# Low parts and taps taken off GpSimd in the recurrence stage, and modulation tasks moved from block 1 to block 1b

## The chip, the core and the metric

The kernel runs on one core of a Trainium2 chip. The metric is the device time of one execution in microseconds. A core has TensorE (PE: matmuls; PEld: its weight loads), VectorE (DVE), ScalarE (ACT), GpSimd (POOL) and SyncE (SP), which issues the DMAs here. Each engine runs its own queue in order, and semaphores join the queues.

## The reference, cut to what matters

Three blocks on a sequence of 512 tokens of 1024 channels, all in float32. The first has a pooling mixer (layer 0) and a dilated attention (layer 1), the second three mixers side by side, the third a bidirectional gated recurrence beside a 31-tap depthwise convolution, and then a convolutional FFN. The parts that the change touches:

```python
# block 1, layer 0: four groups of 512 channels, windows 2, 4, 8, 16
proj = h @ w_in;  u, gate = proj[..., :2048], proj[..., 2048:]
pooled_g = trailing_mean(u_g, w_g) - u_g
mixed_g = pooled_g @ w_grp[g]
y = (mixed * scale * silu(gate)) @ w_out

# modulation vectors: silu(c) @ w + b, for c_ctx_3, c_2 and c_3, eleven vectors of 1024 used in blocks 2 and 3

# block 3: eight heads of 128, in both directions
S_t = diag(f_t) S_{t-1} + k_t v_t^T;  o_t = S_t^T q_t        # in chunks
o = rmsnorm(o) * silu(g);  y_hg = o @ w_hg_out
u = silu(layernorm(dwconv1d(cv_a * sigmoid(cv_b), 31 taps)));  y_cv = u @ w_cv_out
```

## The kernel before, in words

Activations lie transposed: 128 channels on the partitions, 512 tokens along the row. Every product with a weight goes through `form_a` or `form_b`. Each splits weights and activations in a high part (rounded by ScalarE, L129 and L134) and a low part (the rest, a subtraction), and sums three matmuls for each pair of 128-channel tiles, so a `form_a` over 1024 channels is 24 matmuls of 128x512. The subtraction for the weights is L130, on the engine that `k.wlo` names when the weight is asked for: VectorE, or GpSimd in some stretches. Weights come by DMA from SP's queue in three buffers (`wr`), and their parts `wh` and `wl` have three buffers each, so a weight's parts can be made when the product three before has let go of its buffers.

The program is laid out by a scheduler which goes by the order of the code, with the weights' steps ahead by priority, and which may place an instruction of later code earlier where its engine would stand.

**Block 1** runs two halves of two groups each. In a group there are four input products with the trailing means on VectorE (L432 to L438), split into `pg`, then, four times, a gate product (Silu on ScalarE to `sg`) and a group product over `pg`, scaled and gated to `zt` and split into `zh` and `zl`. At the end of each half eight output products run over `z`.

**Modulation tasks** (`vec_input`, `add_vec`) are a list of 102 small jobs: 3 loads of a row vector with its Silu, and 11 vectors of 8 pieces and one finish each. A piece loads 512 KB (`gr`) and multiplies it by the row vector in four quarters on VectorE (L366). `k.bg(n)` takes the next n jobs. Block 1 calls `k.bg(1)` 24 times in each half (4 + 4 in each group, 8 in the output products), and block 1b calls `k.bg(2)` after each head of each attention pass, 32 times, which empties the list in its 27th call. The context steps (`ctx_steps`), which need the first two vectors (the first 19 jobs), begin at the sixth output product of the second half.

**Block 3's recurrence stage.** Ahead of it convolutions c0 to c3 and some products run (`BEFORE`). Then `gla_gates`, `gla_front` and `gla_back` run for heads 0 to 7, with the rest beside them (`BESIDE`: convolutions c4 to c7, gates h0 to h7 and g4 to g7). A head makes exponents of cumulated gates on VectorE and ScalarE, products of 32 to 128 columns on TensorE into `psA` and `psD`, then merges the masked diagonal parts D into A (L1165 to L1171), forms the states SS, the output O, its inverse square root (`rsqrt`, L1212) and the gated result `y`. From L1293 on `k.wlo` is GpSimd, until the last head is done. In c4 to c7 five of the 31 taps run on GpSimd (L1257, L1259), and VectorE adds their sum at the end (L1263).

Of the kernel before, what the change touches and what calls it, by code (L numbers as in the profile page):

```python
# [12 lines left out]
U8 = mybir.dt.uint8  # L13
# [396 lines left out]
def block1(k, ctx, w0, acc, x):  # L410
# [6 lines left out]
    for half in range(2):  # L417
        z = None
        for g in (2 * half, 2 * half + 1):
            w = POOL_W[g]  # L420
            k.wlo = nc.gpsimd if g == 1 else nc.vector
            pg = k.b16(F32R, shape=(P, 2, 4, S), name="pg")
            for m in range(4):
                ps = k.form_a(I["w_in_a"][4 * g + m], x, w=None if g + m else w0)
                u = k.f("upad", (P, PADW + S))
                nc.gpsimd.memset(u[:, :PADW], 0.0)
                nc.scalar.activation(u[:, PADW:], ps, AF.Copy)
                s, sh, lo = u, 1, 0
                while sh < w:
                    lo = lo + sh  # L430
                    s2 = k.f("us", (P, PADW + S))
                    nc.vector.tensor_add(s2[:, lo:], s[:, lo:], s[:, lo - sh:PADW + S - sh])  # L432
                    s, sh = s2, 2 * sh
                pl = k.f("pl")
                nc.vector.scalar_tensor_tensor(pl, s[:, PADW:], 1.0 / w, u[:, PADW:], op0=ALU.mult, op1=ALU.subtract)
                e = k.small((P, 16), "edge")
                nc.vector.tensor_mul(e[:, :w - 1], s[:, PADW:PADW + w - 1], invc[:, :w - 1])
                nc.vector.tensor_sub(pl[:, :w - 1], e[:, :w - 1], u[:, PADW:PADW + w - 1])  # L438
                k.split(pg[:, 0, m], pg[:, 1, m], pl)
                k.bg(1)  # L440
            if z is None:
                z = k.b16(F32R, name="zh"), k.b16(F32R, name="zl")
            for m in range(4):
                ps = k.form_a(I["w_in_a"][16 + 4 * g + m], x)
                sg = k.f("sg")
                end = nc.scalar.activation(sg, ps, AF.Silu)
                ps = k.form_a(I["w_grp_a"][g, m], (pg[:, 0], pg[:, 1]), kt=4)
                t = k.f("zt")
                nc.vector.scalar_tensor_tensor(t, ps, scale_a[:, 4 * g + m:4 * g + m + 1], sg, op0=ALU.mult, op1=ALU.mult)
                kk = 4 * (g % 2) + m  # L450
                k.split(z[0][:, kk], z[1][:, kk], t)
                k.bg(1)
        if half:
            k.table_after(end)
        for j in range(8):
# [9 lines left out]
            k.bg(1)  # L465
# [65 lines left out]
def block1b(k, ctx, acc, h1, x2d):  # L531
# [10 lines left out]
    for j in range(8):  # L542
# [39 lines left out]
        for g in range(2):  # L582
            po = k.ps_o((P, 2, NT, 64))
            ml.append(k.small((P, NT, 4), f"ml{g}"))
            with k.tc.high_priority(offset=(ATT_AHEAD, 0)[g]):
                for hh in range(2):
# [45 lines left out]
                    k.bg(2)  # L632
# [489 lines left out]
def gla_back(k, h, hT, V, R, q, tot, masks, gnw, DB, y):  # L1122
# [40 lines left out]
    m = lambda i, r=slice(0, P): masks[r, i:i + 1, :].to_broadcast([r.stop - r.start, NT, 32])  # L1163
# [6 lines left out]
    for b in range(4):  # L1170
        cp(A[sub(b), :, sub(b)], m(4, sub(b)), D[sub(b)])  # L1171
# [40 lines left out]
    r = k.rsqrt(ss, NT, 1.0 / P, EPS)  # L1212
# [10 lines left out]
def block3(k, hT, x3d, out):  # L1223
# [4 lines left out]
    masks = k.const.tile([P, 5, 32], U8, name="masks")  # L1228
    mf = k.f("mf", (P, 5, 32))
# [13 lines left out]
    def conv(j):  # L1243
# [8 lines left out]
        npt = 5 if j >= 4 else 0  # L1252
        if npt:
            d = k.a("cd")
            for i, t in enumerate(range(31 - npt, 31)):
                e = k.f("ce") if i else d
                nc.gpsimd.tensor_scalar(e, u[:, t:t + S], dww[:, j, t:t + 1], 0.0, op0=ALU.mult, op1=ALU.add)  # L1257
                if i:
                    nc.gpsimd.tensor_add(d, d, e)  # L1259
        for t in range(1, 31 - npt):  # L1260
            nc.vector.scalar_tensor_tensor(c, u[:, t:t + S], dww[:, j, t:t + 1], c, op0=ALU.mult, op1=ALU.add)  # L1261
        if npt:
            nc.vector.tensor_add(c, c, d)  # L1263
# [29 lines left out]
    k.wlo = nc.gpsimd  # L1293
# [149 lines left out]
def constants():  # L1443
# [19 lines left out]
    out["masks"] = np.stack([same(16) & ~same(8), same(8) & ~same(4), same(4) & (si <= ti), same(4) & (si >= ti), same(16)], 1).astype(f)  # L1463
# [83 lines left out]
```

## Time and profile before

| | us |
|---|---|
| median of 3 runs | 3278.64 (3277.37 to 3281.38) |
| the profiled execution | 3281.25 |
| its span, from the first to the last instruction | 3279.2 |
| TensorE busy | 3129.3 |
| VectorE busy | 2109.7 |
| ScalarE busy | 1234.2 |
| GpSimd busy | 452.1 |

All times from the trace count from the start of the span. A busy TensorE is not one at its peak: PEclk is the clock that it was granted, as a share of the full one. A group's mean covers what an instruction took from its start to its end, so time in which it was held up after its start is in it.

### The profile page before, as it was taken

The page shows a single profiled execution, that of the slowest core. Times are in us where ns is not written, and L with a number is a line of the kernel's source. Part 1 is how long each engine was busy: PE and PEld are TensorE (multiplying, and loading weights), DVE is VectorE, ACT ScalarE, POOL GpSimd, SP SyncE. Part 2 cuts the span into 40 slices and gives each one's busy share as a digit, 9 for nine tenths or more (in the row PEclk, how much of TensorE's full clock was granted, in tenths as well). Part 3 has the DMA queues.
Part 4 walks back from the last instruction along what each step waited for, and adds up shares of the span by engine and source line. Part 5 has one row for each costly group of instructions (what it writes and reads, how often), then busy time and mean ns, then how long its engine had stood idle before and what let it go on. Part 6 is the DMA issues. An engine that isn't in the chain of part 4 may idle for free.

```text
span 3279.2 us, 44923 instructions
## 1 busy us (share of the span) xinstructions
PE 3129.3 (95%) x17460; PEld 2567.1 (78%) x17460; DVE 2109.7 (64%) x4077; ACT 1234.2 (38%) x2085; POOL 452.1 (14%) x372
## 2 busy tenths in 40 slices
PE   9799999999999899999999999989879888989998
PEld 7688878787877787777778988888666666878886
DVE  8846764646454735545443363699887788788777
ACT  4233543434343533334442233432454351433332
POOL 1300000000000301100110011221422433110000
PEclk9899999999999999999999999999899999999999
DMA  8523342333222431211122222433212213423332
GB/s 289 197 96 123 112 133 97 127 102 124 96 94 67 122 99 65 67 62 65 52 81 96 91 90 97 135 122 113 70 65 72 82 54 126 151 75 96 97 94 84
DMA packets 112772, 334.35 MB, mean 102 GB/s; under 512 B 17584, under 2 KB 22704, under 8 KB 112560
## 3 DMA queue, kind: packets, MB, share of 16 engines
q1 hardware_dynamic: 112560, 331.50, 30.6%
q8 instruction: 137, 2.24, 0.3%
q14 instruction: 75, 0.61, 0.1%
HBM read 316.77 MB, written 14.68 MB: 101 GB/s over the span
## 4 chain that ended last, share of the span: by engine, by line
PE 39%; DVE 14%; issue 2%; ACT 1%; DVEq 0%; ACTq 0%
PE mm L145 11%; PE mm L144 11%; PE mm L143 11%; DVE cy L1261 5%; PE O L883 1%; DVE wl L130 1%; PE S L867 1%; PE S L1159 1%; PE T L876 1%; PE mm L172 1%; PE mm L174 1%; PE mm L173 1%; DVE KD L1136 0%; DVE A L1171 0%; DVE R L1110 0%
## 5 line engine op out<-in xcount | busy, mean ns | idle before, releaser
L129 ACT ACTIVATE wh<-wr 128x1024 fp32r<-128x1024 f32 (+3 forms) x505 | 504.2, 1000 | 1107.5 <-PE mm L144 798.9
L130 DVE TENSOR_TENSOR wl<-wr,wh 128x1024 fp32r<-128x1024 f32 (+2 forms) x403 | 484.9, 1204 | 422.4 <-ACT wh L129 418.6
L130 POOL TENSOR_TENSOR wl<-wr,wh 128x1024 fp32r<-128x1024 f32 x102 | 257.6, 2530 | 697.5 <-ACT wh L129 652.5
L143 PE MATMUL mm<-h2h,wh 128*128 128x512 f32 (+1 forms) x776 | 310.0, 400 | 1.0 <-ACT th L675 0.9
L145 PE MATMUL mm<-h2h,wl 128*128 128x512 f32 (+1 forms) x776 | 309.8, 399 | 0.0
L144 PE MATMUL mm<-h2l,wh 128*128 128x512 f32 (+1 forms) x776 | 309.6, 399 | 0.0
L144 PE MATMUL mm<-h1l,wh 128*128 128x512 f32 x512 | 212.6, 415 | 1.7 <-DVE h1l L318 1.4
L143 PE MATMUL mm<-h1h,wh 128*128 128x512 f32 x512 | 206.8, 404 | 0.5 <-ACT h1h L317 0.5
L145 PE MATMUL mm<-h1h,wl 128*128 128x512 f32 x512 | 207.0, 404 | 0.0
L144 PE MATMUL mm<-h3l,wh 128*128 128x512 f32 x512 | 204.6, 412 | 1.5 <-DVE h3l L318 1.5
L143 PE MATMUL mm<-h3h,wh 128*128 128x512 f32 x512 | 204.6, 413 | 1.4 <-DVE kk L1001 1.4
L145 PE MATMUL mm<-h3h,wl 128*128 128x512 f32 x512 | 205.5, 414 | 0.0
L1261 DVE SCALAR_TENSOR_TENSOR cy<-uc,dww,cy 128x512 f32<-128x512 f32 x220 | 200.1, 915 | 4.5
L143 PEld LDWEIGHTS mm<-h2h,wh 128*128 128x128 f32 (+1 forms) x776 | 146.0, 188 | 27.7 <-ACT th L675 1.5
L144 PEld LDWEIGHTS mm<-h2l,wh 128*128 128x128 f32 (+1 forms) x776 | 146.1, 188 | 26.1
L145 PEld LDWEIGHTS mm<-h2h,wl 128*128 128x128 f32 (+1 forms) x776 | 145.9, 188 | 25.2
L366 DVE CUSTOM_DVE_ANT_0 gr<-gr,crow 128x256 f32<-128x256 f32 x352 | 158.1, 498 | 9.2 <-DMA gr<-in_w_mod 6.1
L143 PE MATMUL mm<-h4h,wh 128*128 128x512 f32 (+1 forms) x368 | 140.6, 383 | 0.2 <-DVE fc L1375 0.2
L145 PE MATMUL mm<-h4h,wl 128*128 128x512 f32 (+1 forms) x368 | 140.7, 383 | 0.0
L144 PE MATMUL mm<-h4l,wh 128*128 128x512 f32 (+1 forms) x368 | 140.6, 382 | 0.0
L1372 DVE SCALAR_TENSOR_TENSOR fc<-up,fdw,fc 128x512 f32<-128x512 f32 x176 | 131.9, 751 | 4.9
L144 PEld LDWEIGHTS mm<-h3l,wh 128*128 128x128 f32 x512 | 100.2, 196 | 21.8 <-DVE h3l L318 1.9
(524 smaller groups left out, 7366.8 us busy)
## 6 DMA issues: line engine op xcount, KB each, us to landing
gr<-in_w_mod SPq DMA_DIRECT2D x64, 512.0 KB, 4.4
wr<-in_w_up SPq DMA_DIRECT2D x44, 512.0 KB, 3.5
wr<-in_w_in_a SPq DMA_DIRECT2D x32, 512.0 KB, 3.6
wr<-in_w_f SPq DMA_DIRECT2D x32, 512.0 KB, 3.5
wr<-in_w_v SPq DMA_DIRECT2D x32, 512.0 KB, 3.7
wr<-in_w_in_b SPq DMA_DIRECT2D x32, 512.0 KB, 3.5
wr<-in_w_a SPq DMA_DIRECT2D x32, 512.0 KB, 3.5
gr<-in_w_ada SPq DMA_DIRECT2D x24, 512.0 KB, 5.3
```

Of the source, the lines that this page charges most:

```text
L129: self.nc.scalar.activation(h, r, AF.Copy)
L130: self.wlo.tensor_sub(l, r, h.bitcast(F32))
L143: mm(ps, lhsT=wh[:, k], rhs=xh[:, k0 + k, tok], start=first and k == 0, stop=False)
L144: mm(ps, lhsT=wh[:, k], rhs=xl[:, k0 + k, tok], start=False, stop=False)
L145: mm(ps, lhsT=wl[:, k], rhs=xh[:, k0 + k, tok], start=False, stop=last and k == kt - 1)
L172: mm(ps, lhsT=sel(xh, k), rhs=wh[:, kk], start=st, stop=False)
L173: mm(ps, lhsT=sel(xh, k), rhs=wl[:, kk], start=False, stop=False)
L174: mm(ps, lhsT=sel(xl, k), rhs=wh[:, kk], start=False, stop=en)
L366: nc.vector.tensor_tensor_reduce(out=r[:, sl], in0=r[:, sl], in1=self.crow[:, sl], scale=1.0, scalar=0.0, op0=ALU.mult, op1=ALU.add, accum ...
L867: nc.tensor.matmul(sps, lhsT=Q2[:, par, n * P:(n + 1) * P], rhs=KK[b][t][:, par, :W], start=t == 0, stop=t == 1)
L1261: nc.vector.scalar_tensor_tensor(c, u[:, t:t + S], dww[:, j, t:t + 1], c, op0=ALU.mult, op1=ALU.add)
L1372: nc.vector.scalar_tensor_tensor(c, u[:, a:a + 8, b:b + 64], fw[:, j, t:t + 1], c, op0=ALU.mult, op1=ALU.add)
```

## The change

First, the recurrence stage. `k.wlo` stays on VectorE from the start of the stage, so the 52 weights of 128x1024 in it have their low parts made there. All 31 taps of c4 to c7 run on VectorE (20 more there; 20 multiplications and 16 additions leave GpSimd, and 4 additions VectorE). The `rsqrt` of each head runs on GpSimd, but for its first step: 12 operations on 128x4. The four predicated copies of 32 partitions that put D into A become one of 128 partitions over 4x4x32 elements, with masks made for it on the host (8 in place of 5).

Second, the modulation tasks. `k.bg(half)` takes none in the first half of block 1 and one in the second, and block 1b takes three at a time: 24 jobs in block 1 and 78 in block 1b, whose list is empty in the 26th call. In each group of block 1 the four gate products now stand ahead of the four group products, and four `sg` tiles are alive at a time.

```diff
--- before.py
+++ after.py
@@ -437,19 +437,21 @@
                 nc.vector.tensor_mul(e[:, :w - 1], s[:, PADW:PADW + w - 1], invc[:, :w - 1])
                 nc.vector.tensor_sub(pl[:, :w - 1], e[:, :w - 1], u[:, PADW:PADW + w - 1])
                 k.split(pg[:, 0, m], pg[:, 1, m], pl)
-                k.bg(1)
+                k.bg(half)
             if z is None:
                 z = k.b16(F32R, name="zh"), k.b16(F32R, name="zl")
+            sgs = []
             for m in range(4):
-                ps = k.form_a(I["w_in_a"][16 + 4 * g + m], x)
                 sg = k.f("sg")
-                end = nc.scalar.activation(sg, ps, AF.Silu)
+                end = nc.scalar.activation(sg, k.form_a(I["w_in_a"][16 + 4 * g + m], x), AF.Silu)
+                sgs.append(sg)
+            for m, sg in enumerate(sgs):
                 ps = k.form_a(I["w_grp_a"][g, m], (pg[:, 0], pg[:, 1]), kt=4)
                 t = k.f("zt")
                 nc.vector.scalar_tensor_tensor(t, ps, scale_a[:, 4 * g + m:4 * g + m + 1], sg, op0=ALU.mult, op1=ALU.mult)
                 kk = 4 * (g % 2) + m
                 k.split(z[0][:, kk], z[1][:, kk], t)
-                k.bg(1)
+                k.bg(half)
         if half:
             k.table_after(end)
         for j in range(8):
@@ -462,7 +464,7 @@
             else:
                 nc.vector.tensor_add(a, a, ps)
                 k.ln_stats(st, j, a)
-            k.bg(1)
+            k.bg(half)
     h1 = k.b16(F32R, name="h1h"), k.b16(F32R, name="h1l")
     mean, rstd = k.ln_end(st, LN_EPS)
     for j in range(8):
@@ -629,7 +631,7 @@
                             first = b == 0 or (g == 0 and n == 0)
                             with k.tc.high_priority(offset=0):
                                 nc.tensor.matmul(po[:, hh, n], lhsT=pt[:, 2 * a + b], rhs=rhs, start=first, stop=b == 1)
-                    k.bg(2)
+                    k.bg(3)
             t = k.a("o", (P, NT, 2, 64))
             (nc.scalar.activation(t.rearrange("p n h d -> p h n d"), po, AF.Copy) if g else
              nc.vector.tensor_copy(t.rearrange("p n h d -> p h n d"), po))
@@ -1160,15 +1162,15 @@
     A = k.f("A", (P, NT, P))
     nc.scalar.activation(A, psA, AF.Copy)
     cp = nc.vector.copy_predicated
-    m = lambda i, r=slice(0, P): masks[r, i:i + 1, :].to_broadcast([r.stop - r.start, NT, 32])
+    m = lambda i: masks[:, i:i + 1, :].to_broadcast([P, NT, 32])
     for d in range(2):
         cp(DB[:, d], m(2 + d), psD[:, 2 + d])
     D = k.wk.tile([P, NT, 32], F32, name="D", tag="B", bufs=3)
     nc.vector.tensor_add(D, DB[:, 0], DB[:, 1])
     for i in range(2):
         cp(D, m(i), psD[:, i])
-    for b in range(4):
-        cp(A[sub(b), :, sub(b)], m(4, sub(b)), D[sub(b)])
+
+    cp(A.rearrange("p c (b i) -> p c b i", b=4), masks[:, None, 4:].to_broadcast([P, NT, 4, 32]), D[:, :, None].to_broadcast([P, NT, 4, 32]))
 
     dec = k.small((P, 2, NT), "dec")
     nc.scalar.activation(dec, tot, AF.Exp)
@@ -1209,7 +1211,7 @@
     o = k.f("o3", (P, NT, P))
     for c in range(NT):
         nc.scalar.activation(o[:, c], po[:, c], AF.Square, accum_out=ss[:, c:c + 1])
-    r = k.rsqrt(ss, NT, 1.0 / P, EPS)
+    r = k.rsqrt(ss, NT, 1.0 / P, EPS, nc.gpsimd)
     nc.vector.tensor_mul(o, po, r[:, :, None].to_broadcast([P, NT, P]))
     sg = k.f("sg3")
     k.silu2(sg, k.form_a(I["w_gg3"][h], hT))
@@ -1225,8 +1227,8 @@
     nat = [lambda t, kk, n=n: t[:, kk, n * P:(n + 1) * P] for n in range(NT)]
     rst = k.wk.tile([P, S], F32, name="rst", tag="cR", bufs=1)
     nc.sync.dma_start(out=rst, in_=I["rst"])
-    masks = k.const.tile([P, 5, 32], U8, name="masks")
-    mf = k.f("mf", (P, 5, 32))
+    masks = k.const.tile([P, 8, 32], U8, name="masks")
+    mf = k.f("mf", (P, 8, 32))
     nc.sync.dma_start(out=mf, in_=I["masks"])
     nc.vector.tensor_copy(masks, mf)
     gnw = k.col("gnw", (P, 1))
@@ -1249,18 +1251,8 @@
         nc.vector.scalar_tensor_tensor(u[:, 15:S + 15], th, 1.0, k.form_a(I["w_cva"][j], hT), op0=ALU.add, op1=ALU.mult)
         c = k.a("cy")
         nc.vector.tensor_scalar(c, u[:, :S], dww[:, j, 0:1], dwb[:, j:j + 1], op0=ALU.mult, op1=ALU.add)
-        npt = 5 if j >= 4 else 0
-        if npt:
-            d = k.a("cd")
-            for i, t in enumerate(range(31 - npt, 31)):
-                e = k.f("ce") if i else d
-                nc.gpsimd.tensor_scalar(e, u[:, t:t + S], dww[:, j, t:t + 1], 0.0, op0=ALU.mult, op1=ALU.add)
-                if i:
-                    nc.gpsimd.tensor_add(d, d, e)
-        for t in range(1, 31 - npt):
+        for t in range(1, 31):
             nc.vector.scalar_tensor_tensor(c, u[:, t:t + S], dww[:, j, t:t + 1], c, op0=ALU.mult, op1=ALU.add)
-        if npt:
-            nc.vector.tensor_add(c, c, d)
         late.append([wait[0], lambda: k.ln_stats(bst, j, c)])
         nc.sync.dma_start(out=cyd[:, j], in_=c)
 
@@ -1290,7 +1282,6 @@
     nc.gpsimd.memset(DB, 0.0)
     R = k.b16(shape=(P, 2, 4, S), name="R3")
     y = k.b16(F32R, name="yhgh"), k.b16(F32R, name="yhgl")
-    k.wlo = nc.gpsimd
     q = k.wk.tile([P, 2, S], F32, name="q3", tag="c4", bufs=1)
     gates, tot = gla_gates(k, 0, hT), []
     for j in range(-1, 8):
@@ -1460,7 +1451,8 @@
     out["RC"] = np.where((rel >= 0) & (j < 31), -rel, NEG).astype(f)
     si, ti = np.arange(P)[:, None] % 32, np.arange(32)[None]
     same = lambda n: si // n == ti // n
-    out["masks"] = np.stack([same(16) & ~same(8), same(8) & ~same(4), same(4) & (si <= ti), same(4) & (si >= ti), same(16)], 1).astype(f)
+    own = [same(16) & (p // 32 == b) for b in range(4)]
+    out["masks"] = np.stack([same(16) & ~same(8), same(8) & ~same(4), same(4) & (si <= ti), same(4) & (si >= ti), *own], 1).astype(f)
     out["rst"] = np.repeat((np.arange(S) % P != 0).astype(f)[None], P, 0)
     out["cvalid"] = (p >= 31).astype(f)
     out["R"] = np.stack([r0[:, :P], r0[:, P:], r1, r2], 1).astype(f)
```

## Rows read from the trace of the kernel before

Of each instruction the rows give line, engine, operation, output<-inputs and shapes.

**Rows 1.** The page's first part: busy us, share of the span, instructions.
```profile
PE 3129.3 (95%) x17460; PEld 2567.1 (78%) x17460; DVE 2109.7 (64%) x4077; ACT 1234.2 (38%) x2085; POOL 452.1 (14%) x372
```

**Rows 2.** Windows: us, busy PE PEld DVE ACT POOL, PEclk, DMA, GB/s.
```profile
30.00:80.00 50.00, 50.00 (x222) 41.42 (x221) 46.08 (x161) 16.64 (x23) 9.95 (x6) 1.00 0.81 288
80.00:160.00 80.00, 62.33 (x233) 47.97 (x232) 68.64 (x223) 20.55 (x29) 30.70 (x22) 0.83 0.60 205
```

**Rows 3.** TensorE's waits in 0 to 250 us: in total, times, the longest.
```profile
PE mm L143 <- ACT pg L134: 8.5, 2, 6.0
```

**Rows 4.** Windows of L366 alone (a modulation piece's products) on VectorE.
```profile
20.00:160.00 140.00, 85.83 (x320) 0.90 0.70 244
160.00:400.00 240.00, 0.00 (x0) 1.00 0.34 111
400.00:960.00 560.00, 73.12 (x384) 1.00 0.33 112
```

**Rows 5.** Timeline at 86.4 us: start, duration, instruction; GpSimd, then VectorE.
```profile
86.22 2.50 POOL L130 TENSOR_TENSOR wl<-wr,wh 128x1024 fp32r<-128x1024 f32 x1 [7.72 <-ACT wh L129]
86.43 2.56 DVE L366 CUSTOM_DVE_ANT_0 gr<-gr,crow 128x256 f32<-128x256 f32 x1
```

**Rows 6.** The recurrence stage, 2285 to 2740 us: window, then chain by line.
```profile
2285.00:2740.00 455.00, 392.36 (x3232) 302.26 (x3230) 383.09 (x605) 199.10 (x337) 168.45 (x90) 0.93 0.21 69
by line: DVE cy L1261 16.3%; PE mm L145 10.8%; PE mm L144 10.5%; PE mm L143 10.4%; PE S L1159 4.6%; issue 3.7%; DVE KD L1136 3.0%; DVE A L1171 2.9%; DVE R L1110 2.8%; DVE E L1150 2.6%; DVE E L1153 2.6%; DVE QD L1136 2.0%; DVE SS L1201 1.9%;
```

**Rows 7.** VectorE's groups there by form: busy us, mean ns | idle before.
```profile
L1261 DVE SCALAR_TENSOR_TENSOR cy<-uc,dww,cy 128x512 f32<-128x512 f32 x90 | 94.9, 1054 | 1.9
L1153 DVE TENSOR_TENSOR E<-E,q 128x512 f32<-128x512 f32 x40 | 36.1, 908 | 2.1 <-ACT E L1152 2.1
L1151 DVE TENSOR_TENSOR E<-R 128x512 f32<-128x512 f32 x40 | 27.0, 684 | 0.0
L1110 DVE TENSOR_TENSOR_SCAN R<-rst,sp 128x512 f32<-128x512 f32 x8 | 20.2, 2528 | 0.0
L1112 DVE TENSOR_TENSOR_SCAN R<-sp,rst 128x511 f32<-128x511 f32 x8 | 13.0, 1620 | 0.0
L1136 DVE TENSOR_TENSOR KD<-R 128x512 f32<-128x512 f32 x16 | 17.4, 1092 | 0.0
L1184 DVE TENSOR_TENSOR QI<-QI,q 128x512 f32<-128x512 f32 x16 | 15.3, 957 | 0.4 <-ACT q L1109 0.4
L1171 DVE COPY_PREDICATED A<-masks,D 32x128 f32<-32x128 uint8 x32 | 15.5, 484 | 0.4
L222 DVE TENSOR_SCALAR rs_x<-ss 128x4 f32<-128x4 f32 x8 | 5.0, 626 | 12.9 <-ACT o L1211 12.9
L225 DVE TENSOR_TENSOR rs_a<-rs_y 128x4 f32<-128x4 f32 x8 | 3.5, 431 | 0.0
L223 DVE TENSOR_SCALAR rs_y<-rs_x 128x4 int32<-128x4 int32 x8 | 1.3, 166 | 0.1
```

**Rows 8.** Timeline at 2332 us, VectorE: a scan with GpSimd idle.
```profile
2332.41 1.21 DVE L1112 TENSOR_TENSOR_SCAN R<-sp,rst 128x511 f32<-128x511 f32 x1
```

**Rows 9.** GpSimd's groups in the stage, by form.
```profile
L130 POOL TENSOR_TENSOR wl<-wr,wh 128x1024 fp32r<-128x1024 f32 x49 | 130.1, 2660 | 240.8 <-ACT wh L129 198.1 <-PE mm L145 23.0 <-ACT E L1152 10.5
L1259 POOL TENSOR_TENSOR cd<-cd,ce 128x512 f32<-128x512 f32 x12 | 19.3, 1609 | 0.2
```

**Rows 10.** VectorE's groups in 2180 to 2260 us, ahead of the stage.
```profile
L1261 DVE SCALAR_TENSOR_TENSOR cy<-uc,dww,cy 128x512 f32<-128x512 f32 x82 | 60.8, 750 | 1.7
L130 DVE TENSOR_TENSOR wl<-wr,wh 128x1024 fp32r<-128x1024 f32 x14 | 17.1, 1220 | 0.0
```

**Rows 11.** Block 1b, 400 to 960 us: window, then VectorE's low parts.
```profile
400.00:960.00 560.00, 559.34 (x3089) 450.43 (x3088) 293.46 (x898) 224.59 (x440) 19.23 (x58) 1.00 0.33 112
L130 DVE TENSOR_TENSOR wl<-wr,wh 128x1024 fp32r<-128x1024 f32 x70 | 85.7, 1225 | 94.4 <-ACT wh L129 94.3
```

**Rows 12.** GpSimd in 1072 to 1077 us: one inverse square root (12 operations).
```profile
1072.00:1077.00 5.00, 3.84 (x13) 1.00 0.31 110
```

## The prediction, made before the change was run

> **What bounds the kernel now.** I read the page's busy shares first, then the busy table by windows, TensorE's waits, and VectorE's instructions by form in the two stretches that the diff touches. TensorE is busy 95% of the span [rows 1]: where it runs full at the granted clock 1.00, moving vector work gains nothing, and in block 1b it is full, 559.3 of 560 us [rows 11]. So a gain can only come from stretches where TensorE stands or runs at the lower of its two clock levels. The diff touches two of these.
>
> The first is 80 to 160 us, the first half of block 1. It holds 233 matmul records in 80 us, where 30 to 80 us holds 222 in 50 [rows 2], a rate of 4.44 per us: 233 / 4.44 = 52.5 us of work, so **27.5 us are lost**, 17.7 as idle time (80 - 62.3) and the rest at the lower clock level (1.2 GHz), where the mean granted clock is 0.83. The longest wait named is for the pooled tile `pg` [rows 3], which comes off VectorE's queue, busy 68.6 of the 80 us. Most of that is the modulation pieces of L366: 320 quarter rows (40 pieces) in 20 to 160 us, 85.8 us, and none from 160 to 400 [rows 4].
>
> The second is the recurrence stage, 2285 to 2740 us: TensorE 392.4 of 455 us at a mean clock of 0.93, VectorE 383.1, GpSimd 168.5, and the chain that ends last goes through VectorE's lines and TensorE's products in turn [rows 6]. Neither engine is full; they wait for each other.
>
> **GpSimd holds VectorE up.** A low part of 128x1024 starts on GpSimd at 86.22 and takes 2.50 us; the VectorE product that starts at 86.43 takes 2.56 us, and its end falls with GpSimd's [rows 5]. In the stage the same shows as means: a conv tap takes 1054 ns there and 750 ns just ahead of it, where the low parts are on VectorE [rows 7, 10]; the scan of L1110 2528 ns against 1.21 us in the clear [rows 7, 8].
>
> **The stage, part by part.** Against the 383.1 us of VectorE:
> - Hold-ups that go: taps 90 x (1.054 - 0.750) = 27.4; L1153 40 x (0.908 - 0.684), the neighbour L1151 being the clear value, = 9.0; L1110 8 x (2.528 - 1.21) = 10.5; L1112 8 x (1.620 - 1.21) = 3.3; KD 16 x (1.092 - 0.684) = 6.5; QI 16 x (0.957 - 0.684) = 4.4; L222 8 x (0.626 - 0.166) = 3.7. Together 64.8 [rows 7, 8, 10]. All of it is taken as gone, since GpSimd keeps only memsets and 8 x 12 operations on 128x4.
> - The merged predicated copy: 15.5 us for 32 becomes 8 of 128x512. No row has one of that size; the nearest, an SBUF operation of 128x512, has 0.684 us [rows 7]: 5.5, a saving of 10.0. Bounds: free (15.5 saved) and as dear as the four are now (0); an element costs the other operations of this width the same, so I stay at 10.0.
> - The inverse square root moves: two lines at 3.5 us (L225 and one like it) and seven like L223 at 1.3, 16.1 in all, leave VectorE [rows 7]. On GpSimd one of these took at most 3.84 us for 12 operations [rows 12]. On VectorE the ten steps sit in a busy queue, so the latency is taken as unchanged: 0, between -2 and +4 us for each of 8 heads, of which the last head's alone has no next head to cover it.
> - Added: 49 low parts [rows 9] x 1.220 [rows 10] = 59.8, and in this window 15 of the 20 taps (three of the four convolutions, whose 12 sums on GpSimd stand in rows 9) x 0.750 = 11.3. Together 71.1.
>
> VectorE's sum: 383.1 - 64.8 - 10.0 - 16.1 + 71.1 = 363.3, so **19.8 us less**. If its idle time, 455 - 383 = 72 us, stays what it is, the stage shortens by that much. The lower clock costs up to 0.07 x 455 = 31.9 us [rows 6]; it follows stalls, and I take half of it as returned, 16 us, because the longest stalls are the held-up VectorE operations in the chain: **stage -36**. Bounds: nothing returned and 20 us of new waits (0), or TensorE full at the full clock (-94, below). The five taps that fall behind 2740 us cost 3.8 us and lose their own hold-ups: 0.
>
> **Block 1.** 24 of the 48 task slots go. Their DMA issues leave SP's queue with them, so weight loads stand behind fewer 512 KB transfers. All 40 pieces ran ahead of 160 us although half of them stand in the second half's code [rows 4], so I expect the 20 that stay in block 1 to run early too, from 20 to about 85 us. Then the stretch 80 to 160 us still loses VectorE's 20 later pieces and with them its stalls. The four gates ahead of the four group products put three more full products between the last pooled tile and the first product that needs it, 3 x 24 matmuls / 4.44 = 16 us, against a longest wait of 6.0 [rows 3]. What is late next is TensorE itself. I take **-22** of the 27.5. Bounds: -27, and +5 if the four `sg` tiles held at a time make the next evacuations wait for a buffer; no row shows that, and with the weight order alone at stake I lean to the gain.
>
> **Block 1b.** The other 20 pieces come here: 73.1 us / 48 pieces = 1.52 us each [rows 4], 30 us of VectorE where it has 560 - 293 = 267 us free [rows 11]. Bursts of three instead of two stand 1.5 us longer in front of a score product, in 26 places: between 0 and 40 us. With two at a time TensorE lost 0.7 us of 560, so I take **+2**. The third row vector's Silu moves here too, one load and one pass of ScalarE, which is busy 224.6 of the 560 us [rows 11]: 0.
>
> **Sum.** -36 - 22 + 2 = -56 on the profiled execution, 3281.25 (span 3279.2 plus 2.05 around it): 3225. That execution lies 2.6 above the median 3278.64, so the median becomes **3223**.
>
> **Rivals.**
> - *A. TensorE becomes the stage's bound.* 392.4 - 31.9 = 360.5 us at full clock, 94 less; with block 1, -114: **3164**. For it: VectorE would need only 363. Against: the chain crosses between the engines in each head, and that latency stays. 0.10.
> - *B. Low parts wait at the head of VectorE's queue (ends slower).* A low part needs ACT's high part, which needs a free buffer, which TensorE frees; on VectorE the recurrence's own steps queue behind it. In block 1b such waits are 94.3 us for 70, 1.35 each [rows 11], harmless there because VectorE has time. With 49 in the stage they cost 66 us, and -56 becomes +10: **3289**. It decides from 56 / 49 = 1.14 us per low part on. Against: in 2180 to 2260 us, where VectorE is the busy one, 14 low parts waited 0.0 [rows 10]; the stage's VectorE (84% busy) is nearer to that. 0.10 for a loss, 0.06 for waits that eat just the gain.
> - *C. The hold-ups stay.* Then the stage gets 71.1 us and loses 26 on VectorE: +45, and with block 1 +25: **3304**. Rows 5 speak against it. 0.04. The Trainium skill, "Perfetto Trace Analysis", section "Optimizing Scalar/DVE Operations", says that with VectorE saturated, giving work to ScalarE or even GpSimd may make sense, which would be this case; the same paragraph adds that between VectorE and GpSimd it might not help, as they share a port, and by that half, with which rows 5 agree, the work belongs on VectorE.
> - *D. The tasks don't move enough.* The 20 pieces run with the first groups, and half of block 1's loss stays: -7 in place of -22: **3238**. Rows 4 speak for early pieces; the 20 that leave speak against. 0.10.
> - *E. A shuffled order.* Every queue is laid out anew, and with half the stage's gain (-18) the time is **3241**. 0.10.
>
> **How the numbers follow.** Forecast 0.50, centred on 3223 (its own range 3195 to 3250), A 0.10, B 0.16, C 0.04, D 0.10, E 0.10. A measurement of this kernel tells about 0.2% (6.6 us) from no change. Faster by more: 0.50 + A + D + E = 0.80; within it: 0.06; slower: 0.10 + 0.04 = 0.14. The range 3163 to 3272 takes in all but B and C.
>
> **What would show it.** Right: in the profile after, 80 to 160 us at clock 1.00 with some 350 matmuls; the taps at 0.70 to 0.75 us in the stage and no 2.5 us operation on VectorE; the stage 30 us shorter or more; block 1b at TensorE full. Wrong: low parts on VectorE with idle time in front of them in the stage (B), means unchanged (C), `pg` still in TensorE's waits (D), or TensorE standing in block 1b behind score products.

## The result, and the profile after

The changed kernel takes **3197.48 us** (median of 4 runs, 3195.51 to 3197.71) where the kernel before takes 3278.84: a ratio of **0.975, 95% interval 0.9733 to 0.9767**, 81.4 us less. 3223 was forecast, in a range of 3163 to 3272. The direction and the range held, and one term of the sum was too small: the recurrence stage. That the time falls inside the forecast's own range (3195 to 3250) is in part luck: a second error, the inverse square root, pulls the other way, and without it the kernel takes 3179.73 (root_back, below).

To see where the time went, I compared the same points of the work in both traces: the first or the last TensorE product that reads a given tile.

| point | before, us | after, us | moved by |
|---|---|---|---|
| last product with `z` (end of block 1) | 346.8 | 322.0 | -24.8 |
| last product with `h1` (end of block 1b) | 1011.7 | 991.0 | -20.7 |
| first product with `h3` (block 3 begins) | 2153.9 | 2133.5 | -20.4 |
| first product with `yhgh` (all eight heads done) | 2747.2 | 2655.1 | -92.0 |
| end of the span | 3279.2 | 3193.5 | -85.7 |

The table's names stand for both parts of a tile (`zh` and `zl`, and so on). The windows of the stage below begin 131.1 us behind the first product with `h3` and end 7.2 us ahead of the first with `yhgh`, in both kernels.

So block 1 gave 24.8 us, block 1b took 4.1 back and block 2 0.3, the stage gave 71.6, and what stands behind the stage took 6.3 back. The sum is -85.7 on the profiled executions (3281.25 and 3195.51).

The first view is the page of the kernel after: busy us, share of the span, instructions.

```profile
PE 3090.1 (97%) x17460; PEld 2547.2 (80%) x17460; DVE 2052.4 (64%) x4049; ACT 1242.9 (39%) x2092; POOL 310.8 (10%) x380
```

Against [rows 1], TensorE's busy time falls by 39.2 us for the same 17460 products (the rest of the gain is idle time), and VectorE's by 57.3 although it has taken work over. Work that moved to an engine whose total then falls is the first sign that this engine had been waiting inside its instructions.

The next view is the windows of the kernel after: stretch, busy time of PE, PEld, DVE, ACT and POOL with instructions, granted clock, DMA share, GB/s. They answer [rows 2], [rows 11] and [rows 6]. The stage now runs from 2264.6 to 2648; the last window is what follows it.

```profile
30.00:80.00 50.00, 49.08 (x217) 40.34 (x216) 47.52 (x178) 15.88 (x23) 10.98 (x8) 1.00 0.82 291
80.00:160.00 80.00, 78.97 (x347) 64.75 (x347) 32.72 (x50) 24.32 (x33) 36.95 (x25) 1.00 0.29 99
400.00:960.00 560.00, 557.05 (x3073) 447.53 (x3072) 319.07 (x1053) 227.14 (x442) 23.70 (x58) 1.00 0.37 128
2264.60:2648.00 383.40, 359.44 (x3235) 288.15 (x3234) 333.63 (x555) 204.57 (x342) 43.29 (x98) 0.96 0.25 83
2648.00:2795.00 147.00, 134.34 (x617) 110.08 (x615) 110.46 (x152) 43.85 (x55) 21.31 (x22) 0.97 0.43 143
```

From 80 to 160 us TensorE does 347 products where it did 233, at the full clock. In the stage it does 3235 products in 359.4 us where 3232 took 392.4, and it stands for 24.0 us where it stood for 62.6: 33.0 us off its busy time and 38.6 off its idle time make the 71.6. VectorE is busy for 333.6 us instead of 383.1.

VectorE's groups in that stage by form answer [rows 7]: line, operation, shapes, count | busy us, mean ns | idle time before.

```profile
L1255 DVE SCALAR_TENSOR_TENSOR cy<-uc,dww,cy 128x512 f32<-128x512 f32 x89 | 66.7, 749 | 0.8
L130 DVE TENSOR_TENSOR wl<-wr,wh 128x1024 fp32r<-128x1024 f32 x50 | 60.8, 1222 | 5.8 <-ACT wh L129 5.6
L1152 DVE TENSOR_TENSOR E<-R 128x512 f32<-128x512 f32 x40 | 27.4, 687 | 0.0
L1155 DVE TENSOR_TENSOR E<-E,q 128x512 f32<-128x512 f32 x40 | 27.2, 688 | 0.5 <-ACT E L1154 0.5
L1138 DVE TENSOR_TENSOR KD<-R 128x512 f32<-128x512 f32 x16 | 11.0, 687 | 0.0
L1112 DVE TENSOR_TENSOR_SCAN R<-rst,sp 128x512 f32<-128x512 f32 x8 | 9.8, 1220 | 0.0
L1173 DVE COPY_PREDICATED A<-masks,D 128x512 f32<-128x512 uint8 x8 | 5.9, 739 | 0.0
L1215 DVE TENSOR_TENSOR o<-O,rs_y 128x512 f32<-128x512 f32 x7 | 4.8, 691 | 14.2 <-POOL rs_y L220 10.9 <-POOL uc L1250 3.3
L135 DVE TENSOR_TENSOR yhgl<-sg,yhgh 128x512 fp32r<-128x512 f32 x7 | 4.8, 691 | 1.2 <-ACT yhgh L134 1.2
L1169 DVE TENSOR_TENSOR D<-DB 128x128 f32<-128x128 f32 x8 | 2.3, 285 | 0.0
```

Three things stand here. Every row of 128x512 but the scan has 0.69 to 0.75 us, whichever line issues it, and the long scan has 1.22 instead of 2.53. The low parts, `wl`, waited 5.8 us in all, 0.12 each. And one row has idle time that was 0.1 before: VectorE stands 14.2 us ahead of `o`, which scales a head's output by its inverse square root, and 10.9 of them it waits for GpSimd's `rs_y` (the view puts the other 3.3 down to a GpSimd memset, `uc`). TensorE's waits in the stage and behind it (in total, times, the longest) show the same from the other side.

```profile
PE T L1220 <- DVE o L1215: 12.5, 5, 3.8
PE S L250 <- DVE rs_y L216: 5.8, 1, 5.8
```

The first is the longest entry of the stage now; the second stands behind the stage, where the kernel before waited 4.8 us for the last convolution's sum (`cy`). In the kernel before the longest in the stage were others, of which `A` and `QD` are gone from this list:

```profile
PE O L1205 <- DVE A L1171: 19.0, 5, 8.9
PE S L1143 <- DVE QD L1139: 12.3, 3, 8.3
...
PE T L1218 <- DVE o L1213: 3.0, 1, 3.0
```

### The profile page after: what moved, and what is told of

It is laid out like the page before. It is cut to its first block, busy times and chain, and to the rows that moved or that the text cites. A ratio compares the mean times of both kernels' runs of the same rounds, so it can differ in the third digit from the quotient of the medians.

```text
span 3193.5 us, 44907 instructions
## 1 busy us (share of the span) xinstructions
PE 3090.1 (97%) x17460; PEld 2547.2 (80%) x17460; DVE 2052.4 (64%) x4049; ACT 1242.9 (39%) x2092; POOL 310.8 (10%) x380
## 4 chain that ended last, share of the span: by engine, by line
PE 45%; DVE 6%; ACT 2%; issue 1%; POOL 1%; DVEq 0%; ACTq 0%; POOLq 0%
PE mm L143 12%; PE mm L144 12%; PE mm L145 12%; PE O L885 1%; PE mm L172 1%; PE mm L174 1%; PE mm L173 1%; DVE wl L130 1%; PE S L869 1%; PE T L878 1%; DVE cy L1255 0%; ACT wh L129 0%; PE S L1161 0%; POOL rs_c L226 0%; DVE ss L290 0%
## 5 line engine op out<-in xcount | busy, mean ns | idle before, releaser
L130 DVE TENSOR_TENSOR wl<-wr,wh 128x1024 fp32r<-128x1024 f32 (+2 forms) x455 | 547.7, 1205 | 436.6 <-ACT wh L129 433.1
L1255 DVE SCALAR_TENSOR_TENSOR cy<-uc,dww,cy 128x512 f32<-128x512 f32 x240 | 177.1, 749 | 3.4
L130 POOL TENSOR_TENSOR wl<-wr,wh 128x1024 fp32r<-128x1024 f32 (+1 forms) x50 | 118.3, 2370 | 324.7 <-ACT wh L129 324.6
L366 DVE CUSTOM_DVE_ANT_0 gr<-gr,crow 128x256 f32<-128x256 f32 x352 | 135.7, 440 | 9.5 <-DMA gr<-in_w_mod 6.3
L875 ACT ACTIVATE pe<-sb,nm 128x128 f32<-128x128 f32 (+3 forms) x128 | 71.3, 557 | 119.1 <-DVE nm L872 118.9
```

What stands on the lines that cost most here:

```text
L130: self.wlo.tensor_sub(l, r, h.bitcast(F32))
L366: nc.vector.tensor_tensor_reduce(out=r[:, sl], in0=r[:, sl], in1=self.crow[:, sl], scale=1.0, scalar=0.0, op0=ALU.mult, op1=ALU.add, accum ...
L875: nc.scalar.activation(pe, sb, AF.Exp, bias=m, scale=-1.0, accum_out=lt[:, n, b:b + 1])
```

## The experiments

Each kernel was timed beside the kernel before, whose median was 3278.8 to 3280.8 us from one comparison to the next. The last column is a difference between kernels timed in different comparisons, so 2 us in it say nothing. The sections below take the kernels in the order of the questions; the table has them all.

| kernel | median us | ratio to before, 95% | against after, us |
|---|---|---|---|
| after | 3197.48 | 0.9750 (0.9733 to 0.9767) | |
| tasks_only | 3258.10 | 0.9937 (0.9922 to 0.9952) | +60.6 |
| stage_only | 3216.63 | 0.9809 (0.9793 to 0.9826) | +19.2 |
| moved_only | 3268.02 | 0.9966 (0.9953 to 0.9979) | +70.5 |
| gates_first | 3271.08 | 0.9976 (0.9967 to 0.9985) | +73.6 |
| extra_pool | 3282.49 | 1.0011 (1.0002 to 1.0021) | +85.0 |
| low_back | 3253.99 | 0.9919 (0.9903 to 0.9936) | +56.5 |
| taps_back | 3214.94 | 0.9803 (0.9789 to 0.9818) | +17.5 |
| root_back | 3179.73 | 0.9694 (0.9680 to 0.9709) | -17.8 |
| copies_back | 3197.71 | 0.9749 (0.9734 to 0.9763) | +0.2 |
| none_on_pool | 3159.37 | 0.9632 (0.9618 to 0.9647) | -38.1 |
| conv_early | 3190.98 | 0.9732 (0.9716 to 0.9749) | -6.5 |
| best | 3156.90 | 0.9621 (0.9603 to 0.9638) | -40.6 |

### Do the two changes add up?

tasks_only is the kernel before with the part of the change in blocks 1 and 1b alone:

```diff
-                k.bg(1)
+                k.bg(half)
...
+            sgs = []
             for m in range(4):
-                ps = k.form_a(I["w_in_a"][16 + 4 * g + m], x)
...
-                    k.bg(2)
+                    k.bg(3)
```

> The second half of the change alone (tasks moved, gates first), on the kernel before. If the two halves of the change are independent, the marks of the two traces say 24.8 us less up to the end of block 1 and 4.1 us more in block 1b: 20.4 less in all, 3258 us. If the new layout of the queues ties them together, it is more than 5 us off that.

stage_only is the kernel before with the rest of it: taps, low parts, inverse square root and merged copy.

```diff
-    r = k.rsqrt(ss, NT, 1.0 / P, EPS)
+    r = k.rsqrt(ss, NT, 1.0 / P, EPS, nc.gpsimd)
...
-        npt = 5 if j >= 4 else 0
...
-    k.wlo = nc.gpsimd
```

> The first half of the change alone (recurrence stage). If independent, 85.7 - 20.4 = 65.3 us less than before: 3213 us. My prediction's -36 would be 3243.

Measured: 21.1 us less and 62.6 us less than before. Together 83.7, where the whole change has 81.4: the two parts don't disturb each other by more than these differences can tell. stage_only came out 3.6 us above its forecast. In tasks_only the window of 80 to 160 us is that of the whole change:

```profile
80.00:160.00 80.00, 78.97 (x347) 64.76 (x346) 33.37 (x50) 24.02 (x32) 37.77 (x26) 1.00 0.32 101
```

At the points of the table above, tasks_only has -24.0 for block 1 and +4.3 in block 1b.

### What gained in block 1: the moved tasks or the order of the gates?

moved_only is the kernel before with the task slots moved and the old order of gates and groups:

```diff
-                k.bg(1)
+                k.bg(half)
...
-                    k.bg(2)
+                    k.bg(3)
```

> Tasks moved, gate and group products in the order of before. Theory backlog (VectorE's pieces in front of the pooling steps are what TensorE waits for): nearly all of tasks_only, 3258 to 3263 us. Theory order (the slack of three more gate products is what counts): most of the gain is missing, 3270 us or more.

gates_first is the kernel before with the four gates of a group ahead of its four group products, and the tasks where they were:

```diff
+            sgs = []
             for m in range(4):
-                ps = k.form_a(I["w_in_a"][16 + 4 * g + m], x)
                 sg = k.f("sg")
-                end = nc.scalar.activation(sg, ps, AF.Silu)
+                end = nc.scalar.activation(sg, k.form_a(I["w_in_a"][16 + 4 * g + m], x), AF.Silu)
+                sgs.append(sg)
+            for m, sg in enumerate(sgs):
```

> Gates ahead of the group products, tasks where they were before. Theory backlog: 3270 to 3279 us, since VectorE's queue is as long as before in 80 to 160 us. Theory order: the slack of 16 us covers the waits for pg, 3262 us or less.

Measured: 11.2 us less and 8.1 us less. The first lies between the ranges of the two theories, so neither of them is enough for it; the second lies in the range of the theory of the backlog. Windows of 80 to 160 us and TensorE's longest wait there, first of moved_only, then of gates_first:

```profile
80.00:160.00 80.00, 72.60 (x302) 58.25 (x301) 34.91 (x58) 23.18 (x31) 34.50 (x24) 0.94 0.30 93
...
PE mm L143 <- ACT pg L134: 4.9, 1, 4.9
```

```profile
80.00:160.00 80.00, 67.26 (x265) 52.36 (x265) 63.44 (x210) 21.53 (x30) 32.94 (x23) 0.91 0.58 200
...
PE mm L143 <- DVE zt L451: 6.8, 2, 6.0
```

Neither alone does it. With the tasks gone VectorE is down to 34.9 us, and `pg` is still late by 4.9, because the first group product follows the last pooled tile at once. With the gates first the wait for `pg` is gone, but VectorE is still busy for 63.4 us, and TensorE waits for `zt`, the next tile that comes off its queue (in the kernel before it waited 5.8 us there for `zh`, which is made from `zt`). The two add: 11.2 + 8.1 = 19.3 of the 21.1 us of both.

### Is it the hold-up, or that low parts come late from GpSimd?

After the change GpSimd has almost nothing to do in the stage. That can gain in two ways: VectorE is no longer held up inside its instructions, or TensorE gets its low parts sooner. extra_pool tells them apart: it is the kernel after, in which GpSimd does one more subtraction of 128x1024 behind each low part of the stage, and nothing uses its result.

```diff
+            if self.extra:
+                self.nc.gpsimd.tensor_sub(r, r, h.bitcast(F32))
...
+    k.extra = True
```

> The kernel after, with one more subtraction of 128x1024 on GpSimd behind each of the 52 weights of the stage, made in place in the raw weight that nobody reads any more. No step waits for its value. Theory hold-up (a GpSimd tensor operation holds VectorE's up while it runs): 52 x 2.5 us of GpSimd are back; at the ratio of the kernel before (some 85 us of hold-ups to 168 us of GpSimd) that is 65 us on VectorE, and the stage grows by 40 to 80 us, 3240 to 3280. Theory lateness (the gain came from low parts that are ready sooner, 1.2 in place of 2.7 us): nothing waits for this, 3197 to 3203.

Measured: 3282.49, **85.0 us more than after**, a little above the range of the hold-up theory: some 50 unused subtractions take back all that the whole change gains, 1.7 us each. The stage's window, two of VectorE's groups in it, and GpSimd's own:

```profile
2265.00:2732.00 467.00, 379.45 (x3237) 297.77 (x3236) 428.08 (x561) 204.45 (x342) 178.91 (x149) 0.92 0.21 69
...
L1258 DVE SCALAR_TENSOR_TENSOR cy<-uc,dww,cy 128x512 f32<-128x512 f32 x93 | 101.4, 1090 | 1.0
...
L1158 DVE TENSOR_TENSOR E<-E,q 128x512 f32<-128x512 f32 x40 | 40.0, 1008 | 3.0 <-ACT E L1157 2.9
...
L133 POOL TENSOR_TENSOR wr<-wr,wh 128x1024 f32<-128x1024 f32 x50 | 140.2, 2806 | 233.7 <-DVE wl L131 216.9 <-DVE rs_x L225 12.5 <-DVE R L1116 4.2
```

The tap has 1090 ns and the E product 1008, even more than in [rows 7]. VectorE is busy for 94.5 us more than in the kernel after, with the same work of its own, and idle for 38.9 us; the stage is 83.6 us longer. The lateness theory, under which nothing should have moved, falls.

The trace shows the hold-up instruction by instruction. Of the taps that start in this window, the 29 that overlap one of the unused subtractions in time have a mean of 1.79 us, the other 63 have 0.74. It doesn't strike every operation: none of the 37 operations that read PSUM (TensorE's results) beside a subtraction took over 0.75 us, and the mean of each such line lies within 0.01 us of its mean alone. One other way to lose time was open, since the subtraction writes into `wr` and so holds that buffer longer: SP's queue waits 306.7 us for it in the window, 47 times, where in the kernel after it waits 247.4 us for `wl`, 46 times. But none of TensorE's waits in this window is for `wh` or `wl`, and in the kernel before none in its stage is either.

### What each part of the stage is worth

Four kernels put one part of the stage back as it was, in the kernel after. low_back puts the low parts on GpSimd:

```diff
+    k.wlo = nc.gpsimd
```

> The kernel after, with the stage's 52 low parts on GpSimd again. VectorE loses 60 us of work and gets back hold-ups of about 65 us: by VectorE's sum alone 3200; if the hold-ups fall on the chain of a head, where one of 2.7 us delays both engines, 3230 to 3245. If low parts at the head of VectorE's queue had cost much, it would be faster than after, below 3190.

taps_back gives the last five taps of four convolutions to GpSimd:

```diff
-        for t in range(1, 31):
+        npt = 5 if j >= 4 else 0
...
+        for t in range(1, 31 - npt):
```

> The kernel after, with five taps of c4 to c7 on GpSimd again: 50 us of GpSimd back, 15 us less work on VectorE, some 25 us of hold-ups: 3203 to 3215. If a tap on GpSimd is truly off VectorE: 3185.

root_back has the inverse square root on VectorE:

```diff
-    r = k.rsqrt(ss, NT, 1.0 / P, EPS, nc.gpsimd)
+    r = k.rsqrt(ss, NT, 1.0 / P, EPS)
```

> The kernel after, with the inverse square roots on VectorE again: 8 x 10 operations of 0.16 us, 13 us, back on VectorE, where they queue; against it the 11 us that VectorE's step behind it waited for GpSimd. 3194 to 3206; if GpSimd's latency were what the stage's end now hangs on, 3190 or less.

copies_back has four predicated copies in place of the merged one:

```diff
-    cp(A.rearrange("p c (b i) -> p c b i", b=4), masks[:, None, 4:].to_broadcast([P, NT, 4, 32]), D[:, :, None].to_broadcast([P, NT, 4, 32]))
+    for b in range(4):
+        cp(A[sub(b), :, sub(b)], masks[sub(b), 4 + b:5 + b, :].to_broadcast([32, NT, 32]), D[sub(b)])
```

> The kernel after, with four predicated copies of 32 partitions in place of the merged one. By durations 8 x (4 x 0.29 - 0.74) = 3.4 us more on VectorE, right ahead of the output product in the chain: 3198 to 3203 us. If merging had cost something (the wait for all of A at once), below 3196.

Measured against after: the low parts are worth 56.5 us and the taps 17.5; the merged copy is worth 0.2, which is nothing that can be told apart; and the inverse square root on GpSimd **costs 17.8**. 56.5 + 17.5 + 0.2 - 17.8 = 56.4, near the 60.6 us that the stage part adds to tasks_only (3258.10 - 3197.48). taps_back lies in its range and copies_back just below its own. The low parts missed their expectation upwards; one thing that it left out is that they stand in GpSimd's queue beside the square root's steps, and VectorE's wait for `rs_y` grows from 10.9 to 20.8 us. How much of the miss that is was not tried. root_back is far below the 3194 to 3206 expected for it, on the side of its alternative, that the stage hangs on GpSimd's latency. The window of low_back, two of its groups:

```profile
2264.00:2716.00 452.00, 392.71 (x3221) 302.17 (x3220) 357.35 (x518) 199.41 (x337) 159.28 (x158) 0.92 0.21 69
...
L1255 DVE SCALAR_TENSOR_TENSOR cy<-uc,dww,cy 128x512 f32<-128x512 f32 x99 | 96.3, 972 | 2.2
...
L130 POOL TENSOR_TENSOR wl<-wr,wh 128x1024 fp32r<-128x1024 f32 x48 | 123.1, 2570 | 225.2 <-ACT wh L129 175.9 <-PE mm L145 35.2 <-issue 14.1
```

VectorE has 49 low parts fewer, some 59.9 us by 1.222 each, and yet it is busy for 23.7 us *more* than in the kernel after. Ten more taps lie in this window, some 7.5 us by 0.749 each; the other 16 us, and the 59.9, are hold-ups. Giving work away made the engine busier.

Where the square root's loss comes from, the kernel after shows in two stretches of its timeline (start, duration, instruction). First GpSimd's first steps at 2319 us, where VectorE is between two waits, then at 2470 us, and what VectorE does there:

```profile
2319.58 0.20 POOL L223 TENSOR_SCALAR rs_y<-rs_x 128x4 int32<-128x4 int32 x1 [70.77 <-DVE rs_x L222]
2319.86 0.20 POOL L226 TENSOR_SCALAR rs_c<-rs_x 128x4 f32<-128x4 f32 x1
...
2470.00 2.98 POOL L223 TENSOR_SCALAR rs_y<-rs_x 128x4 int32<-128x4 int32 x1 [51.29 <-DVE rs_x L222]
2473.05 0.19 POOL L226 TENSOR_SCALAR rs_c<-rs_x 128x4 f32<-128x4 f32 x1
...
2469.96 0.69 DVE L1152 TENSOR_TENSOR E<-R 128x512 f32<-128x512 f32 x1
2470.56 2.36 DVE L130 TENSOR_TENSOR wl<-wr,wh 128x1024 fp32r<-128x1024 f32 x2
```

The same operation on 128x4 takes 0.20 us in one head and 2.98 in another, and that one ends at 2472.98, 0.06 us behind the second of VectorE's two low parts. The hold-up works in both directions: a small GpSimd operation waits for VectorE's large ones. In the stage L226 has a mean of 1.27 us over eight heads, and 4.8 at the most (at 2610.85):

```profile
L226 POOL TENSOR_SCALAR rs_c<-rs_x 128x4 f32<-128x4 f32 x8 | 10.2, 1270 | 0.6
```

And in root_back, the window, one of the steps on VectorE, `o`, and TensorE's wait for it:

```profile
2264.60:2630.00 365.40, 353.63 (x3215) 282.19 (x3214) 335.16 (x613) 201.88 (x331) 3.40 (x9) 0.99 0.26 86
...
L225 DVE TENSOR_TENSOR rs_a<-rs_y 128x4 f32<-128x4 f32 x7 | 1.1, 158 | 0.0
...
L1215 DVE TENSOR_TENSOR o<-O,rs_y 128x512 f32<-128x512 f32 x7 | 4.8, 683 | 0.0
...
PE T L1220 <- DVE o L1215: 0.6, 2, 0.4
```

A step takes 0.16 us on VectorE; the ten steps are some 1.6 us per head. On GpSimd there are also more of them: `rsqrt` splits three of its fused steps in two there, so nine steps that leave VectorE become 12. The 14.2 us ahead of `o` and the 12.5 us of TensorE's wait are gone, and the stage has 365.4 us.

### Where it leads

If GpSimd's work beside a busy VectorE costs in the stage, it should cost elsewhere too. none_on_pool is root_back with every low part of the whole kernel on VectorE, and with block 1b's own inverse square root:

```diff
-        self.wlo = self.nc.gpsimd
+        self.wlo = self.nc.vector
...
-    mean, rstd = k.ln_end(st, LN_EPS, nc.gpsimd)
+    mean, rstd = k.ln_end(st, LN_EPS)
```

> The kernel of root_back (3179.7), with every low part on VectorE in the whole kernel (some 50 more) and the inverse square root at the end of block 1b there too. Theory hold-up alone: a further 5 to 20 us less, since 118 us of GpSimd stood in block 1 and around the stage borders, 3160 to 3175. Theory balance (at the borders, where VectorE does the normalisation, GpSimd's low parts were off the path): block 1 unchanged, the borders 2 to 8 us slower each, 3180 to 3200. The marks of the trace give each border by itself.

Measured: 3159.37, another 20.4 us less than root_back. By the points of the work 3.4 of it lies in block 1, some 9 at the border from block 1b to 2, 4.5 at the next border and 3 in the stage. The first border has both edits, low parts and square root, and no run tells which gave the 9.

conv_early is root_back with the last convolutions one or two heads earlier, so that c7 would not end behind the last head, and with task bursts of two and three in turn in block 1b:

```diff
-                    k.bg(3)
+                    k.bg(2 + hh)
...
-BESIDE = ("c4 h0 g4", "h1 g5", "h2", "c5 h3 g6", "h4 g7", "h5", "c6 h6", "h7 c7")
+BESIDE = ("c4 h0 g4", "h1 g5", "c5 h2", "h3 g6", "c6 h4 g7", "h5", "c7 h6", "h7")
```

> The kernel of root_back, with convolutions c5 to c7 begun one or two heads earlier and block 1b taking two and three tasks in turn (80 in 32 calls). If the 6 to 8 us that TensorE stands behind the last convolution's statistics after the stage are owed to its late place, 3168 to 3174; if VectorE's sum is what counts there, 3177 to 3182. In block 1b, if bursts of three cost the 4 us, 2 us of them come back.

Measured: 3190.98, 11.3 us *more* than root_back; both theories missed. Windows of block 1b and the stage:

```profile
400.00:960.00 560.00, 559.16 (x3092) 449.87 (x3091) 315.71 (x1026) 227.95 (x446) 18.26 (x56) 1.00 0.38 127
2258.00:2642.00 384.00, 364.26 (x3212) 290.87 (x3210) 349.64 (x628) 198.44 (x327) 3.51 (x11) 0.96 0.25 83
```

The shorter bursts won 5.5 us in block 1b (TensorE 559.2 of 560 busy where the kernel after has 557.1), but the stage became 17 longer. VectorE has 14.5 us more to do inside it than in root_back (107 taps where root_back has 86), which accounts for most of that if VectorE sets the pace there; that it does was not shown, and the cause stays open. From the first product with `yhgh` to the end, where fewer taps are left, only 0.7 us came back.

best is none_on_pool with those bursts and the old order of convolutions:

```diff
-                    k.bg(3)
+                    k.bg(2 + hh)
```

> The kernel of none_on_pool (3159.4) with two and three tasks in turn in block 1b. In conv_early block 1b was 5.5 us shorter with it; if bursts of three are what costs there, the same here: 3152 to 3156. If those 5.5 us were the other edit's doing, 3158 to 3161.

Measured: **3156.90**, 0.9621 (0.9603 to 0.9638) of the kernel before and 40.6 us less than after. Block 1b is 5.2 us shorter, and 3.4 of these are lost again in block 2, for which no run here has a reason; the median lies between the two ranges expected, and its interval overlaps that of none_on_pool.

## Why the prediction was right, and where it was not

**What bounds.** Right: the gain came from the two stretches named and from nowhere else, and the two parts add (21.1 + 62.6 against 81.4).

**Hold-ups.** Right, and now shown: VectorE's counted groups came to the values that were taken as clear ones, the taps 749 ns (750 forecast), L1155 688 (684), the scan 1220 (1210), KD 687 (684), and extra_pool brings hold-ups back with work that nothing needs. Rival C falls with it. Of the two halves of the Trainium skill's rule cited with it ("Perfetto Trace Analysis", section "Optimizing Scalar/DVE Operations"), the runs bear out the second, that moving work between VectorE and GpSimd might not help: in low_back VectorE gave its low parts away, and its busy time rose.

**The stage's term was too small:** -36 forecast, -71.6 measured. VectorE's sum was 29.7 us short (-19.8 forecast, 383.1 - 333.6 = -49.5 measured), in two places. The first is the taps: 15 more were counted into the stage, and it has one fewer (89 against 90), since 13 taps of c6 now lie behind the last head and three more of c3's ahead of the stage; that is 12.1 us, some of which is only moved. The second is the list of hold-ups: it left out groups that were held up too. Against [rows 7] and the rest of that view, yhgl fell from 8.4 to 4.8, the sum D from 6.5 to 2.3, R of L1114 (now L1116) from 7.7 to 5.5, the E product now at L1152 from 29.5 to 27.4, with smaller ones some 13 us; and the three additions of L1263, 2.1 us, left VectorE without standing in the sum. The wrong step was to list the groups with a visible neighbour as clear value, and to take the others as clear already. The rest of the list was right within 0.7 us a line, the added low parts among them (50 at 1.222, one of which was there before).

**Idle time and clock.** The sum held VectorE's idle time at 72 us and gave back half of the slow clock, 16 us. Idle time fell to 49.8, so 22.1 us came from these two together, 6 more than forecast. By the granted clock itself the forecast of half was good: the stage has 0.96 now, which by the same reckoning costs 0.04 x 383.4 = 15.3 us where it was 31.9, so 16.6 came back. TensorE's busy time for the same products fell by more, 33.0 us, and where the rest of that comes from is not shown. That the shorter idle time and the higher clock can't be had one without the other is likely, but no run here tells them apart.

**The inverse square root: the step that failed.** Its latency was taken as unchanged, with bounds of -2 to +4 us per head of which only the last head's would count. It costs 17.8 us. Two errors met. The price on VectorE, 16.1 us for eight heads, was read from held-up rows, 3.5 us for L225, which in the clear has 158 ns (1.1 us for seven); and GpSimd's price was read from [rows 12], outside the stage, where VectorE let it run. In the stage each head's square root stands between two TensorE steps, and TensorE waited for it five times, not in the last head alone.

**The merged copy.** The number was right (15.5 us became 5.9, -9.6 against -10.0), its reason was not. In copies_back, with GpSimd out of the way, the four copies have 294 ns each, 9.4 us for 32, so 6.1 us of the term were hold-up that goes without any merging, and the merging itself saves 3.5 us of VectorE. Of those the clock shows nothing that can be told apart (0.2 us): a term of VectorE's busy time is not a term of the end.

**The five taps behind the stage: 0 forecast.** The stretch behind it took 6.3 us back. In the kernel before, the 25 taps of the last convolution stood there; now its 30 do and 13 of the one ahead of it. TensorE waits 5.8 us for the normalization that follows, where it waited 4.8 for `cy` before. That the later taps are the cause is not shown: taps_back, with five taps of each convolution on GpSimd again, takes back 11.3 us there, and conv_early, with fewer taps left there, 7.0.

**Block 1.** -22 forecast, -24.8 measured, and TensorE at 347 products from 80 to 160 us as forecast (some 350). The mechanism was told as two reasons of which the order of the gates alone should cover the wait for `pg`; gates_first shows that the wait then moves to `zt`, and moved_only that `pg` stays late without it. Rival D falls: of the 704 records of L366, 160 run ahead of 160 us (320 in [rows 4]), 16 up to 400 us, and 528 in block 1b. (A quarter of a piece leaves two records, the product and the reading of its sum, so the prediction's 320 quarter rows are 160; its 40 pieces are right.) The view is that of [rows 4], of the kernel after.

```profile
20.00:160.00 140.00, 33.99 (x160) 1.00 0.52 184
160.00:400.00 240.00, 3.02 (x16) 1.00 0.34 114
400.00:960.00 560.00, 99.47 (x528) 1.00 0.37 128
```

**Block 1b.** +2 forecast, +4.1 measured. The reason given, three pieces ahead of a score product, is borne out: with two and three in turn 5.2 to 5.5 us come back, and TensorE's wait ahead of score products in 400 to 960 us (for `qk`) goes from 2.2 us to 0.2 in conv_early.

**The rivals.** B, the low parts waiting at the head of VectorE's queue, fell at 0.12 us each where 1.14 would have decided. A, TensorE as the stage's bound, did not come in the kernel after (383.4 us where A had 360.5), but root_back, with the square root back on VectorE, comes near: 365.4 us, of which TensorE is busy for 353.6. E, a shuffled order, is not seen in the change itself; conv_early, whose order of convolutions was changed, is 11.3 us slower than root_back, with the cause open.

## What to carry to other kernels

Where GpSimd and VectorE are busy at the same time, read VectorE's means by form against a stretch in which GpSimd stands: the excess of *all* groups is what GpSimd's work costs VectorE, and an engine's own busy time is no measure of what it can spare. Price every operation from rows in the clear before it is moved, and a short chain of small operations from rows beside the work that will run next to it: on the path, ten steps of 0.16 us on a busy VectorE beat a chain of 12 on a GpSimd that had little else to do. When a sum counts busy time, ask of each term whether the path goes through it: two terms of 10 and 16 us here were worth 0 and less than 0, and more than half of the first was hold-up counted as work.

## What the runs showed of the hardware that was not expected

- The hold-up goes both ways. On 128x4 a GpSimd operation takes 0.20 us in the clear, 1.27 as a mean of one line in the stage, and 4.8 at the most. At 2470 us it stood for 2.98 us, through a VectorE product of 0.69 us and two low parts in a row. The Trainium skill, "SBUF — State Buffer", section "SBUF: two separate sides", says that VectorE and GpSimd share a pair of ports as an exclusive lock: a GpSimd operation, or one of VectorE that runs in a two-port mode or has two inputs in SBUF, holds it for its whole instruction if it starts first, while the other is blocked. The trace agrees on the lock, and extra_pool's operations that read PSUM, 37 of them beside a subtraction and none stretched by it, fit the condition; that the one that waits may be blocked through several instructions in succession, as at 2470 us, is more than that sentence says.
- GpSimd work that nothing needs is not free: some 50 subtractions of 128x1024 cost 85.0 us, 1.7 each, more than the 1.22 us that the same subtraction takes on VectorE.
